# Attention: how wide the value products are, and where they stand

## The chip, the cores and the metric

The kernel runs on one core of a Trainium2 chip. The metric is the device time of one execution in microseconds (us), lower is better. PE is the core's matrix engine, DVE the vector engine, ACT the scalar engine, POOL the general engine, and SP issues most of the transfers (DMAs). A "product" below is one matmul instruction of PE.

## The reference

A decoder trunk of two layers on x of 1024 tokens by 1024 channels: layer 0 mixes by a short gated convolution, layer 1 by dilated attention, and each layer ends with a SwiGLU network. The change touches layer 1's mixer only:

```python
qkv = (h @ w_qkv).reshape(bsz, seq, 3, N_HEADS, HEAD_DIM)
q, k, v = qkv[:, :, 0], qkv[:, :, 1], qkv[:, :, 2]
for window, dilation in BRANCHES:          # (128, 1), (512, 4), (2048, 16)
    o, l = dilated_branch(q, k, v, rel_bias, window, dilation)
...
o = jnp.sum(alpha[..., None] * jnp.stack(outs, axis=0), axis=0)
return o.reshape(bsz, seq, D_MODEL).astype(h.dtype) @ w_out
```

There are 16 heads of 64 channels. Each query sees keys of three strides, with a bias by distance and a softmax over all of them. The part of the change is `v`: h (1024 by 1024) times the last third of `w_qkv` (1024 by 1024).

## The kernel before

**Numbers.** Operands are split into a high part and a low remainder, and each product of two matrices is made of three matmuls: hi times hi, hi times lo, lo times hi. A weight slab is loaded raw by SP (L153), ACT copies the high part (L139), DVE subtracts it for the low part (L140). Each is needed by its first product. SBUF is handed out in pages of 128 partitions by 1024 floats from a pool of 41 in rotation; a new tile waits for the last reader of the page that it takes.

**Order.** Nothing reorders instructions: each engine runs its own in the order in which the program writes them, and waits by semaphores for the others. The order in which weights are loaded and split is a list (`ops`); `take(key)` splits up to that key and looks a number of raw slabs ahead.

**Attention.** The normalized input h lies as eight tiles of 128 channels, each with a high and a low part. Heads go in pairs, p = 0 to 7, and the values in groups of four heads (256 columns), g = 0 to 3.

A prologue makes the keys and queries of pair 0 (`qkv(0, first=True)`) and the values of group 0 (`value_tiles(0, 0)` and `(0, 1)`). Then come slots n = 0 to 16 (`slot`), one per head and one more. Slot n makes the scores of head n (L1464, L1465) beside the products of weights with values of head n - 1 (`values`, L1537). After these, ACT evicts z and o (L1560, L1561). An odd slot (the second head of a pair) then splits the keys and queries of the next pair (`split_kq`: ACT copies to ka, kb, qa, qb, kca and kcb, L1433, and DVE's remainders, L1432). An even slot loads the values of its own pair from memory (`load_values`, L1420 and L1422, to vx). The softmax of head n is written about half way down this second part: POOL's all-reduce of the maxima (L1518) comes with the scores, then DVE subtracts (L1526) and ACT takes the exponentials (L1527) of lf, lh, ld and lp. Slot n + 1 begins with scores, and its first product with values needs lf.

Between these a slot calls `next(dense)` a set number of times, `ndense`, 27 in most slots. `dense` is the generator `qkv(p + 1)`: 36 steps for the keys and queries of the next pair (four products over eight input tiles, a step being three matmuls of 512 columns, L360 to L362, and one step for each eviction), and then steps for values: a step is six matmuls of 256 columns (L1403 to L1405), every fifth step is an eviction by ACT (L1408). At the end of an odd slot `run(dense)` drains what is left.

**Values before.** `value_tiles(g, j)` makes four tiles of 128 tokens by 256 columns, each 24 matmuls. Group 0 stands in the prologue (192 matmuls). The pairs 0 to 5 carry half a group each (96 matmuls): p = 0 and 1 group 1, 2 and 3 group 2, 4 and 5 group 3, with two weight slabs taken at each group's first half. Each page of four tiles is written to memory (`vdram`, L1412) by four DMAs on SP.

Of the kernel before, what the change touches and what calls it, by code (L numbers as in the profile page):

```python
# [3 lines left out]

# [8 lines left out]
AF = mybir.ActivationFunctionType  # L13
# [8 lines left out]
KT = D // 128  # L22
FT = DF // 128
HALF = 512
NPAIR = H // 2
# [65 lines left out]
def view(t, off, dims):  # L91
    return bass.AP(tensor=t.tensor, offset=t.offset + off, ap=[t.ap[0]] + [list(d) for d in dims])
# [3 lines left out]
def trunk(ctx: ExitStack, tc: tile.TileContext, x, gains_in, cwi, ck, cwo, wqkv, wo, relb,  # L96
          wg, wu, wd, oneh, ident, out):
    nc = tc.nc
# [6 lines left out]
    def page(name, dt=F32):  # L105
        return pages.tile([128, 1024], dt, name=name, tag="page", bufs=PAGES)
# [22 lines left out]
    def split(src, dst=None, eng=nc.vector):  # L129

        w = src.shape[1]
        if dst is None:
            if w <= HALF:
                t = page("w", F32R)
                dst = t[:, :w], t[:, HALF:HALF + w]
            else:
                dst = page("w_hi", F32R)[:, :w], page("w_lo", F32R)[:, :w]
        hi, lo = dst
        nc.scalar.activation(hi, src, AF.Copy)  # L139
        eng.tensor_tensor(out=lo, in0=src, in1=hi, op=ALU.subtract)  # L140
        return hi, lo
# [3 lines left out]
    raw_src, raw_tile, raw_state = [], {}, [0]  # L145
    ops, made, op_state = [], {}, [0, 0]
    combos, raw_base, sums_of = {}, {}, {}

    def load_raw(upto):
        while raw_state[0] < min(upto + 1, len(raw_src)):  # L150
            i = raw_state[0]
            raw_tile[i] = page("raw")
            nc.sync.dma_start(raw_tile[i][:, :raw_src[i].shape[1]], raw_src[i])  # L153
            raw_state[0] += 1

    def get_raw(i, ahead=2):
        load_raw(i + ahead)
        return raw_tile[i]
# [9 lines left out]
    def take(key, ahead=1):  # L168
        i = op_state[1]
        assert ops[i][0] == key, (ops[i][0], key)  # L170
        ensure(i + ahead)
        op_state[1] += 1
        return made.pop(i)

    def add_slab(key, src):
        i = len(raw_src)
        raw_src.append(src)
        ops.append((key, lambda: split(get_raw(i)[:, :src.shape[1]])))

    def add_pair(u, rows, w, eng, upto, low=()):  # L180

# [155 lines left out]
    for p in range(NPAIR):  # L337
        for part in (1, 0):
            add_slab(("qkv", p, part), wqkv[part * KT + p])
        if p == 0 or p % 2 and p < NPAIR - 1:  # L340
            for j in range(2):
                add_slab(("v", (p + 1) // 2, j), wqkv[2 * KT + (p + 1) // 2 * 2 + j])
    for g in range(2):
        for n in range(KT):
            add_slab(("ao", g, n), wo[n][:, g * AO * 128:(AO * 128, D)[g]])
# [996 lines left out]
        return (j // 4) * HALF + (j % 4) * 8  # L1342

    def attention(norm):
        KS, KC, QS, wv = {}, {}, {}, []

        qlo = [scope["pool"].tile([128, S], F32R, name=f"ql{a}") for a in range(2)]
        for a in range(2):
# [43 lines left out]
        def value_tiles(g, j):  # L1392

            if j == 0:
                wv[:] = [take(("v", g, i), 1) for i in range(2)]
            v = page("v")
            for b4 in range(4):
                t = 4 * j + b4
                b = bank()[:, :256]
                for k in range(KT):  # L1400
                    (hi, lo), (whi, wlo) = norm.h[k], wv[k // 4]
                    a, c = slice(t * 128, t * 128 + 128), slice(k % 4 * 256, k % 4 * 256 + 256)
                    nc.tensor.matmul(b, hi[:, a], whi[:, c], start=k == 0, stop=False)  # L1403
                    nc.tensor.matmul(b, hi[:, a], wlo[:, c], start=False, stop=False)  # L1404
                    nc.tensor.matmul(b, lo[:, a], whi[:, c], start=False, stop=k == KT - 1)  # L1405
                    if k % 2:
                        yield
                nc.scalar.activation(v[:, b4 * 256:b4 * 256 + 256], b, AF.Identity, scale=norm.r[:, t:t + 1])  # L1408
                yield
            vd = vdram[g]  # L1410
            for r in range(4):
                nc.sync.dma_start(bass.AP(vd.tensor, vd.offset + (512 * j + r) * 256,  # L1412
                                          [[16 * 256, 32], [4 * 256, 4], [1, 256]]), v[32 * r:32 * r + 32])

        def load_values(p):
            src = vdram[p // 2]
# [346 lines left out]
    with tc.tile_pool(name="first", bufs=1) as scope["pool"]:  # L1763
# [4 lines left out]
        norm = Norm(1)  # L1768
# [11 lines left out]
    with tc.tile_pool(name="third", bufs=1) as scope["pool"]:  # L1780
# [3 lines left out]
        norm = Norm(4)  # L1784
# [135 lines left out]
```

## Time and profile before

| | |
|---|---|
| median of 3 runs | 2162.24 us (2159.44 to 2163.09) |
| the profiled execution | 2161.95 us |
| its span in the trace | 2159.9 us |
| its mean granted PE clock | 0.994 |
| value products ahead of slot 0 | 192 of 256 columns |
| value products in pairs 0 to 5 | 576 of 256 columns |

The profile is of one execution of its own, so durations are compared with its time, 2161.95, which is 2 us more than the span that the trace covers. In the page's rows "x" counts instructions and "out<-in" names the tiles. A timeline row is start, duration, engine, line, operation, tiles, shapes, and in brackets the idle time just before with what ended it. A row of busy time by stretches has the stretch and its length, busy time of PE, PE's weight loads, DVE, ACT and POOL with counts, then PE's granted clock (1.00 is full), the DMA share and GB/s; where it is of one line alone, only the engines of that line stand in it.

### The profile page before, as it was taken

How to read it: one execution, taken by the hardware profiler on the slowest of the kernel's cores; microseconds unless marked ns; L12 is line 12 of the kernel's file. 1: busy time of each engine (PE TensorE's matmuls, PEld its weight loads, DVE VectorE, ACT ScalarE, POOL GpSimd, SP SyncE). 2: the span in 40 equal slices, each digit the busy share in tenths (PEclk: the TensorE clock that was granted, in tenths of full speed). 3: DMA queues.
4: the chain of work that ended last, by engine and by line, in shares of the span. 5: the costliest groups of instructions: out<-in, count | busy, mean ns of one | idle time of the engine just before them, and what ended most of it. 6: DMA issues, size and time to landing. Idle time of an engine off the chain costs nothing.

```text
span 2159.9 us, 30731 instructions
## 1 busy us (share of the span) xinstructions
PE 2128.0 (99%) x11086; PEld 1819.9 (84%) x11086; DVE 1735.9 (80%) x3166; ACT 996.4 (46%) x1792; POOL 217.7 (10%) x308
## 2 busy tenths in 40 slices
PE   8999999999999999999999999999999999999998
PEld 6788878888888888878999999887788888888887
DVE  7798758988898888865777777769988888888886
ACT  7433426444444433445455555525544444434435
POOL 2000001111211100010111111110011211200000
PEclk9999999999999999999999999999999999999999
DMA  7222543334455684323333333534224554586432
GB/s 211 69 93 67 213 150 88 127 106 163 165 173 175 233 325 145 112 64 129 92 93 93 93 93 85 172 120 167 79 88 142 175 173 164 171 317 225 160 93 79
DMA packets 148066, 306.71 MB, mean 142 GB/s; under 512 B 49850, under 2 KB 61130, under 8 KB 147914
## 3 DMA queue, kind: packets, MB, share of 16 engines
q1 hardware_dynamic: 82026, 206.83, 29.4%
q0 software_dynamic: 24720, 74.83, 10.0%
q10 hardware_dynamic: 41168, 23.10, 3.5%
q8 instruction: 88, 1.44, 0.3%
q14 instruction: 64, 0.52, 0.1%
HBM read 209.06 MB, written 88.28 MB: 138 GB/s over the span
## 4 chain that ended last, share of the span: by engine, by line
PE 86%; DVE 6%; ACT 4%; issue 2%; DMA 2%; ACTq 0%; SPq 0%; DVEq 0%
PE bank L566 18%; PE bank L567 18%; PE bank L568 18%; PE bank L362 5%; PE bank L360 5%; PE bank L361 5%; PE bank L1537 4%; PE bank L659 2%; PE bank L662 2%; PE bank L661 2%; PE bank L1465 1%; PE bank L1464 1%; PE bank L1405 1%; PE bank L1404 1%; PE bank L1403 1%
## 5 line engine op out<-in xcount | busy, mean ns | idle before, releaser
L566 PE MATMUL bank<-b,w 128*128 128x512 f32 x1816 | 712.6, 392 | 7.5 <-ACT part L572 6.7
L567 PE MATMUL bank<-b,w 128*128 128x512 f32 x1816 | 709.9, 391 | 0.6 <-DVE b L905 0.6
L568 PE MATMUL bank<-b,w 128*128 128x512 f32 x1816 | 709.0, 390 | 1.1 <-DVE w L140 1.1
L566 PEld LDWEIGHTS bank<-b,w 128*128 128x128 f32 x1816 | 342.7, 189 | 82.3 <-ACT part L572 9.0
L568 PEld LDWEIGHTS bank<-b,w 128*128 128x128 f32 x1816 | 342.3, 189 | 73.8 <-DVE w L140 2.3
L567 PEld LDWEIGHTS bank<-b,w 128*128 128x128 f32 x1816 | 342.6, 189 | 70.9 <-DVE b L905 1.2
L139 ACT ACTIVATE w<-combo 128x512 fp32r<-128x512 f32 (+2 forms) x448 | 229.3, 539 | 255.3 <-DVE combo L187 254.4
L140 DVE TENSOR_TENSOR w<-combo,w 128x512 fp32r<-128x512 f32 (+2 forms) x448 | 254.7, 581 | 27.5 <-ACT w L139 27.1
L572 ACT ACTIVATE part<-bank 128x512 f32<-128x512 f32 x168 | 100.2, 597 | 301.3 <-PE bank L568 284.9
L140 DVE TENSOR_TENSOR w<-raw,w 128x512 fp32r<-128x512 f32 (+2 forms) x312 | 172.0, 570 | 25.6 <-ACT w L139 25.3
L576 DVE TENSOR_TENSOR part<-part,bank 128x256 f32<-128x256 f32 (+1 forms) x328 | 154.2, 500 | 40.0 <-ACT part L572 26.7
L139 ACT ACTIVATE w<-raw 128x512 fp32r<-128x512 f32 (+2 forms) x312 | 152.8, 527 | 61.3 <-DMA raw<-in_ffn_w_down 16.5
L820 DVE TENSOR_TENSOR x<-x,bank 128x512 f32<-128x512 f32 x168 | 114.8, 684 | 37.4 <-PE bank L568 33.6
L360 PE MATMUL bank<-w_hi,w 128*128 128x512 f32 (+1 forms) x320 | 119.8, 374 | 2.1 <-ACT w L139 2.1
L362 PE MATMUL bank<-w_hi,w 128*128 128x512 f32 (+1 forms) x320 | 118.1, 369 | 0.7 <-DVE w L140 0.7
L361 PE MATMUL bank<-w_lo,w 128*128 128x512 f32 (+1 forms) x320 | 117.8, 368 | 0.0
L497 DVE TENSOR_TENSOR x<-x,bank 128x512 f32<-128x512 f32 (+1 forms) x104 | 66.0, 642 | 60.5 <-PE bank L362 52.2
L360 PE MATMUL bank<-h_hi,w_hi 128*128 128x512 f32 x256 | 104.5, 408 | 0.3 <-ACT w_hi L139 0.3
L187 DVE TENSOR_TENSOR combo<-raw 128x512 f32<-128x512 f32 (+1 forms) x160 | 103.2, 645 | 0.0
L362 PE MATMUL bank<-h_hi,w_lo 128*128 128x512 f32 x256 | 100.1, 391 | 0.7 <-DVE w_lo L140 0.7
L361 PE MATMUL bank<-h_lo,w_hi 128*128 128x512 f32 x256 | 99.9, 390 | 0.0
L1518 POOL PARTITION_ALL_REDUCE mb<-m x16 | 51.5, 3222 | 422.0 <-DVE m L1515 161.4
(259 smaller groups left out, 3798.9 us busy)
## 6 DMA issues: line engine op xcount, KB each, us to landing
hin<-part SPq DMA_DIRECT2D x126, 256.0 KB
raw<-in_ffn_w_gate SPq DMA_DIRECT2D x44, 512.0 KB
raw<-in_ffn_w_up SPq DMA_DIRECT2D x44, 512.0 KB
b<-ready SPq DMA_DIRECT2D x42, 512.0 KB
part<-sum POOLq DMA_DIRECT2D x72, 256.0 KB, 3.5
raw<-in_ffn_w_down SPq DMA_DIRECT2D x48, 384.0 KB
x<-spill SPq DMA_DIRECT2D x24, 512.0 KB
raw<-in_attn_w_qkv SPq DMA_DIRECT2D x24, 512.0 KB
```

What stands on the lines that cost most here:

```text
L139: nc.scalar.activation(hi, src, AF.Copy)
L140: eng.tensor_tensor(out=lo, in0=src, in1=hi, op=ALU.subtract)
L187: eng.tensor_tensor(out=c, in0=a, in1=b, op=op)
L360: nc.tensor.matmul(b, whi[:, a], ahi[:, s], start=first, stop=False)
L361: nc.tensor.matmul(b, whi[:, a], alo[:, s], start=False, stop=False)
L362: nc.tensor.matmul(b, wlo[:, a], ahi[:, s], start=False, stop=last)
L566: nc.tensor.matmul(b, hi[:, a], bhi, start=start and k == 0, stop=False, skip_group_check=True)
L567: nc.tensor.matmul(b, hi[:, a], blo, start=False, stop=False, skip_group_check=True)
L568: nc.tensor.matmul(b, lo[:, a], bhi, start=False, stop=k == n - 1, skip_group_check=True)
L572: nc.scalar.activation(t, b, AF.Copy)
L576: nc.vector.tensor_tensor(out=t, in0=t, in1=b, op=ALU.add)
L820: nc.vector.tensor_tensor(out=X[n][:, half(h)], in0=X[n][:, half(h)], in1=b, op=ALU.add)
```

## The change

Three things are changed.

Groups 0 and 1 (heads 0 to 7) are both made in the prologue, in one product of 512 columns: `wide_values` has eight tiles of 128 tokens, each 24 matmuls, with a weight slab of two input tiles by 512 columns. There are four of these slabs, each loaded by two DMAs. Each tile has one eviction of 512 columns, and two tiles fill a page, which eight DMAs write to `vdram`.

Groups 2 and 3 (heads 8 to 15) are spread over the pairs: `value_tiles(g)` is one generator for a whole group, and the run of pair p = 1 to 6 (in the slots of pair p - 1) takes 15 steps of it, that is 3, 3 and 2 tiles for each group. The weights are taken at p = 1 and p = 4.

`ndense` goes from 27 to 25 in both slots of pairs 0 to 5.

```diff
-        if p == 0 or p % 2 and p < NPAIR - 1:
+        if p == 0:
+            for j in range(4):
+                add_wide(("v", 0, j), [wqkv[2 * KT + g * 2 + j // 2][:, j % 2 * HALF:j % 2 * HALF + HALF]
+                                       for g in range(2)])
+        if p in (1, 4):
             for j in range(2):
-                add_slab(("v", (p + 1) // 2, j), wqkv[2 * KT + (p + 1) // 2 * 2 + j])
+                add_slab(("v", 2 + p // 4, j), wqkv[2 * KT + (2 + p // 4) * 2 + j])
...
             if first:
-                yield from value_tiles(0, 0)
-            n = p - 1
-            if first or n < NPAIR - 2:
-                yield from value_tiles(0 if first else n // 2 + 1, 1 if first else n % 2)
+                yield from wide_values()
+            elif p < NPAIR - 1:
+                if p % 3 == 1:
+                    tiles[0] = value_tiles(2 + p // 4)
+                yield from islice(tiles[0], 15)
+
+        def wide_values():
+
+            w = [take(("v", 0, i), 1) for i in range(4)]
+            for t in range(8):
+                b = bank()
+                v = page("v") if t % 2 == 0 else v
+                for k in range(KT):
+                    (hi, lo), (whi, wlo) = norm.h[k], w[k // 2]
+                    a, c = slice(t * 128, t * 128 + 128), half(k % 2)
+                    nc.tensor.matmul(b, hi[:, a], whi[:, c], start=k == 0, stop=False)
+                    nc.tensor.matmul(b, hi[:, a], wlo[:, c], start=False, stop=False)
+                    nc.tensor.matmul(b, lo[:, a], whi[:, c], start=False, stop=k == KT - 1)
+                    yield
+                nc.scalar.activation(v[:, half(t % 2)], b, AF.Identity, scale=norm.r[:, t:t + 1])
+                if t % 2:
+                    for r in range(4):
+                        for g in range(2):
...
+                            nc.sync.dma_start(bass.AP(vd.tensor, vd.offset + row * 256,
+                                                      [[16 * 256, 32], [4 * 256, 2], [1, 256]]),
+                                              view(v[32 * r:32 * r + 32], g * 256, [[HALF, 2], [1, 256]]))
+                yield
...
-            slot(2 * p, dense, 24 if last else 29 if p == NPAIR - 2 else 27, 3 if last else 0, hook)
+            slot(2 * p, dense, 24 if last else 29 if p == NPAIR - 2 else 25, 3 if last else 0, hook)
             run(hook)
-            slot(2 * p + 1, dense, 22 if last else 27)
+            slot(2 * p + 1, dense, 22 if last else 27 if p == NPAIR - 2 else 25)
```

How the order moves on ACT in the prologue, from the first splits of pair 0's keys and queries. In brackets stand the semaphores waited for (DMA queues, DVE, PE, ACT itself, Pool for POOL); w_hi is the high part of a weight slab. Before:

```order
L1433 ACTIVATE qa<-kq 64x512 [waits DMAHW7_49,DVE_49]
L1433 ACTIVATE qb<-kq 64x512 [waits DMAHW0_49]
L139 ACTIVATE w_hi<-raw 128x1024 [waits DMAHW6_49]
L1433 ACTIVATE qa<-kq 64x512
L1433 ACTIVATE qb<-kq 64x512
```

And with the change, whose split_kq is L1474:

```order
L1474 ACTIVATE qa<-kq 64x512 [waits DMAHW1_49,DVE_49]
L1474 ACTIVATE qb<-kq 64x512 [waits DMAHW2_49]
L139 ACTIVATE w_hi<-raw 128x1024 [waits DMAHW1_49,DMAHW0_49]
L139 ACTIVATE w_hi<-raw 128x1024 [waits DMAHW5_49,DMAHW3_49,DMAHW2_49]
L139 ACTIVATE w_hi<-raw 128x1024 [waits DMAHW4_49,DMASW1_49,Activation_49]
L1474 ACTIVATE qa<-kq 64x512
L1474 ACTIVATE qb<-kq 64x512
```

Where one weight slab stood behind the first four copies, three do: slabs 2 and 3 of the wide product, and the next pair's first.

ACT in the odd slot of pair 1 (slot 3), from the first split copy behind the evictions to the first exponential. Before:

```order
L1433 ACTIVATE qa<-kq 64x512 [waits DVE_49,Activation_49]
L1433 ACTIVATE qb<-kq 64x512 [waits Pool_49]
L1433 ACTIVATE qa<-kq 64x512
...
L1433 ACTIVATE qb<-kq 64x512
L1408 ACTIVATE v<-bank,r 128x256 [waits DMAHW1_49,DMAHW6_49,DVE_49,PE_49]
L1433 ACTIVATE qa<-kq 64x512
L1433 ACTIVATE qb<-kq 64x512
L1433 ACTIVATE kca<-ka 128x512 [waits DVE_49]
L1433 ACTIVATE kcb<-kb 128x512 [waits DVE_49]
L1527 ACTIVATE lf<-lf 128x1024 [waits DVE_49]
```

And with the change, where the exponentials are L1568:

```order
L1474 ACTIVATE qa<-kq 64x512 [waits Activation_49,Pool_49]
L1474 ACTIVATE qb<-kq 64x512 [waits PE_49]
L1474 ACTIVATE qa<-kq 64x512
...
L1474 ACTIVATE qb<-kq 64x512
L1474 ACTIVATE qa<-kq 64x512
L1474 ACTIVATE qb<-kq 64x512
L1474 ACTIVATE kca<-ka 128x512 [waits DVE_49]
L1474 ACTIVATE kcb<-kb 128x512 [waits DVE_49]
L1568 ACTIVATE lf<-lf 128x1024 [waits DVE_49]
```

The eviction of a value tile that stood among the copies now stands behind the exponentials, and the wait for POOL has moved from qb to qa, one copy earlier.

More of the change, by code (lines that the diff above doesn't have):

```diff
@@ L1 @@
 import math
-from itertools import chain
+from itertools import chain, islice
 from contextlib import ExitStack
@@ L147, in trunk, with load_one @@
     combos, raw_base, sums_of = {}, {}, {}
+    def load_one(i):
+        raw_tile[i] = page("raw")
+        src = raw_src[i]
+        if isinstance(src, list):
+            for g, s in enumerate(src):
+                nc.sync.dma_start(view(raw_tile[i], g * 256, [[HALF, 2], [1, 256]]),
+                                  bass.AP(s.tensor, s.offset, [s.ap[0], [256, 2], [1, 256]]))
+            return
+        nc.sync.dma_start(raw_tile[i][:, :src.shape[1]], src)
     def load_raw(upto):
         while raw_state[0] < min(upto + 1, len(raw_src)):
-            i = raw_state[0]
-            raw_tile[i] = page("raw")
-            nc.sync.dma_start(raw_tile[i][:, :raw_src[i].shape[1]], raw_src[i])
+            load_one(raw_state[0])
             raw_state[0] += 1
@@ L1386, in qkv, with value_tiles @@
             if first:
-                yield from value_tiles(0, 0)
-            n = p - 1
-            if first or n < NPAIR - 2:
-                yield from value_tiles(0 if first else n // 2 + 1, 1 if first else n % 2)
[L1392 to L1398, printed above, removed]
+                yield from wide_values()
[19 more added lines that the diff above has]
+                        for g in range(2):
+                            vd = vdram[g]
+                            row = 512 * (t // 4) + 4 * (t % 4 - 1) + r
+                            nc.sync.dma_start(bass.AP(vd.tensor, vd.offset + row * 256,
+                                                      [[16 * 256, 32], [4 * 256, 2], [1, 256]]),
+                                              view(v[32 * r:32 * r + 32], g * 256, [[HALF, 2], [1, 256]]))
+                yield
+        def value_tiles(g):
+            wv = [take(("v", g, i), 1) for i in range(2)]
+            for t in range(8):
+                j, b4 = divmod(t, 4)
+                v = page("v") if b4 == 0 else v
                 b = bank()[:, :256]
@@ L1408, in value_tiles @@
                 nc.scalar.activation(v[:, b4 * 256:b4 * 256 + 256], b, AF.Identity, scale=norm.r[:, t:t + 1])
+                vd = vdram[g]
+                for r in range(4 * (b4 == 3)):
+                    nc.sync.dma_start(bass.AP(vd.tensor, vd.offset + (512 * j + r) * 256,
+                                              [[16 * 256, 32], [4 * 256, 4], [1, 256]]), v[32 * r:32 * r + 32])
                 yield
[L1410 to L1413, printed above, removed]
         def load_values(p):
```

6 lines of the change are left out of this document (5 added, 1 removed).

## The prediction

> **What bounds the kernel now.** I read the page first, then busy time by stretches, then the timelines of PE, ACT and POOL around the places where values are computed.
>
> ```profile
> span 2159.9 us, 30731 instructions
> PE 2128.0 (99%) x11086; PEld 1819.9 (84%) x11086; DVE 1735.9 (80%) x3166; ACT 996.4 (46%) x1792; POOL 217.7 (10%) x308
> ...
> PE 86%; DVE 6%; ACT 4%; issue 2%; DMA 2%; ACTq 0%; SPq 0%; DVEq 0%
> ```
>
> PE is busy for 99% of the span and holds 86% of the chain that ended last; ACT is busy for under half and still holds 4% of it. So two questions decide: how many us of PE work the change adds or removes, and whether PE still has work wherever something is taken from it. The attention part shows the price of a value product (stretches of the 256 column products alone, a third of them: line L1403 is one of the three lines of each product):
>
> ```profile
> 1007.30:1030.80 23.50, 18.50 (x64) 12.28 (x64) 1.00 0.10 23
> 1120.00:1131.70 11.70, 9.05 (x32) 6.00 (x32) 1.00 0.12 46
> ```
>
> The first row is the prologue ahead of slot 0: 3 x 64 = 192 products. The second is slot 3: 3 x 32 = 96. Slot 3 is an odd slot, and its end, from the last product of the values with the weights (L1537) to the first of the next slot, reads so on PE:
>
> ```profile
> 1116.60 0.47 PE L360 MATMUL bank<-h_hi,w_hi 128*128 128x512 f32 x1
> 1116.91 0.39 PE L361 MATMUL bank<-h_lo,w_hi 128*128 128x512 f32 x1
> ...
> 1119.86 0.39 PE L362 MATMUL bank<-h_hi,w_lo 128*128 128x512 f32 x1
> 1120.09 0.28 PE L1403 MATMUL bank<-w_hi,h_hi 128*128 128x256 f32 x1
> ...
> 1131.48 0.28 PE L1405 MATMUL bank<-w_hi,h_lo 128*128 128x256 f32 x1
> ...
> 1132.30 0.28 PE L1464 MATMUL bank<-qa,kca 128*128 128x256 f32 x1
> ...
> 1132.99 1.16 PE L1537 MATMUL bank<-lf,vx 128*128 128x128 f32 x8
> ```
>
> and on ACT and POOL:
>
> ```profile
> 1118.63 0.63 ACT L1433 ACTIVATE kb<-kq 64x512 fp32r<-64x512 f32 x1
> 1119.28 0.63 ACT L1433 ACTIVATE qa<-kq 64x512 fp32r<-64x512 f32 x1
> 1121.34 0.63 ACT L1433 ACTIVATE qb<-kq 64x512 fp32r<-64x512 f32 x1 [1.43 <-POOL mb L1518]
> ...
> 1127.98 0.47 ACT L1408 ACTIVATE v<-bank,r 128x256 f32<-128x256 f32 x1
> ...
> 1131.88 1.05 ACT L1527 ACTIVATE lf<-lf 128x1024 f32<-128x1024 f32 x1
> ```
> ```profile
> 1118.08 3.23 POOL L1518 PARTITION_ALL_REDUCE mb<-m  x1 [22.28 <-DVE m L1515]
> ```
>
> The first exponential ends at 1131.88 + 1.05 = 1132.93, and PE's first product that needs it starts at 1132.99. ACT has gone from the last product's eviction through the split copies of keys and queries to that exponential with a single wait (1.43 us for POOL's all-reduce). So the end of an odd slot has two limits of equal length: PE's products and ACT's row of copies. Taking PE work out of it gains nothing that ACT doesn't give up as well.
>
> **What a product costs, narrow and wide.** 96 products of 256 columns go from 1120.09 to 1131.60 (the last starts at 1131.48 and takes one step): 11.51 us, 0.120 each. From the first L361 at 1116.91 to the last L362 of that stretch at 1119.86 lie 13 steps of 512 columns (five triples, of which these are the second and the fifteenth): 2.95 us, 0.227 each. So two narrow ones cost 0.240 and a wide one 0.227. The change turns 384 narrow ones (groups 0 and 1) into 192 wide ones: 46.1 against 43.6 us, a saving of 2.5 us in all, 0.1%. The Trainium skill, "Perfetto Trace Analysis", section on optimizing tensor performance, says of matmuls that larger ones are more efficient where possible; the rows agree, but by 5% only.
>
> **Prologue: +20.5 us of PE work, and a new wait of 3.3.** Before, 192 narrow products, 23.04 us; now 192 wide ones, 43.58 us, and nothing runs beside them that leaves the path: +20.5. Their evictions (ACT, one of 512 columns per token tile) and writes hide beside the products. The splits of the weight slabs do not. The order of ACT puts the high parts of slabs 2 and 3 behind four split copies, where one slab stood before; that slab's rows, and the first value product:
>
> ```profile
> 1007.44 0.68 PE L1403 MATMUL bank<-w_hi,h_hi 128*128 128x256 f32 x1
> ```
> ```profile
> 1011.07 0.63 ACT L1433 ACTIVATE qb<-kq 64x512 fp32r<-64x512 f32 x1
> 1011.72 1.06 ACT L139 ACTIVATE w_hi<-raw 128x1024 fp32r<-128x1024 f32 x1
> ```
> ```profile
> 1012.81 1.23 DVE L140 TENSOR_TENSOR w_lo<-raw,w_hi 128x1024 fp32r<-128x1024 f32 x1 [1.84 <-ACT w_hi L139]
> ```
>
> A wide slab holds two of the eight input tiles, so slab 2 is due after 12 products. The first starts at 1007.44 and takes 0.40 longer than the usual 0.28 of the L1403 row above; then 12 x 0.227 gives 1010.57. Its low part is there at 1012.81 + 1.23 = 1014.04. One product (hi times hi) fits in between, so PE waits 3.47 - 0.23 = 3.25 us. Slab 3 follows one split later, at about 1015.3, and is due at 1016.8: no wait. Bounds: 0, if the splits come to stand earlier than the copies before them allow; 4.5, if slab 3 costs another split of 1.23.
>
> Slot 0 then needs the values back from memory. The writes on SP's queue are eight per two tiles, not four per four:
>
> ```profile
> 1024.51 2.58 SPq L1412 DMA_DIRECT2D vdram<-v  x4
> ```
> ```profile
> 1045.61 1.06 ACT L1527 ACTIVATE lf<-lf 128x1024 f32<-128x1024 f32 x1 [1.33 <-DVE lf L1526]
> ```
> ```profile
> 1051.52 0.72 PE L1537 MATMUL bank<-lf,vx 128*128 128x128 f32 x5
> ```
>
> At 0.65 us each the last group takes 2.6 longer, while the first exponential of slot 0 ends 1051.52 - 1046.67 = 4.85 ahead of its use. This costs nothing; the bound if the cover were gone is 2.6.
>
> **Slots: 23.0 us of products leave, 8.6 come back.** Pairs 0 to 5 lose 24, 24, 48, 24, 24, 48 narrow products (3, 3, 2, 3, 3, 2 tiles where 4 were), 192 in all, 23.0 us. All of them leave the end of an odd slot, since the generator is drained there. The numbers 27 to 25 work the other way: a slot takes two steps less, one eviction step and one step of three products. So 3 x 0.227 = 0.68 us leaves the even slot and 0.68 the first part of the odd one, and six products move to the odd slot's end. Each of the twelve slots is bound by PE where these stand: -8.2 us that are real.
>
> The odd slots' ends before: slot 3 has 1132.99 - 1116.60 = 16.39. Slot 1 reads
>
> ```profile
> 1062.82 0.47 PE L360 MATMUL bank<-h_hi,w_hi 128*128 128x512 f32 x1
> ...
> 1078.99 0.38 PE L1537 MATMUL bank<-lf,vx 128*128 128x128 f32 x2
> ```
> ```profile
> 1070.22 1.04 ACT L139 ACTIVATE w_hi<-raw 128x1024 fp32r<-128x1024 f32 x1
> ...
> 1077.66 1.05 ACT L1527 ACTIVATE lf<-lf 128x1024 f32<-128x1024 f32 x1
> ```
>
> 16.17, bound by PE; ACT's row there, with a weight split and no wait for POOL, ends at 1078.71, so alone it would give 15.95 (with the 0.06 from exponential to product). Slots 5 and 9 I take to be like slot 1, slots 7 and 11 like slot 3: 3 x 16.17 + 3 x 16.39 = 97.7.
>
> After: PE's own work is 16.17 + 6 x 0.227 - 24 x 0.120 = 14.65 with three tiles and 11.77 with two. ACT's row loses the value eviction (0.47), which now comes behind the exponentials. In pairs 1, 2, 4 and 5 it keeps the wait for POOL, and by the order the copy that waits is qa and not qb: the all-reduce ends at the same time and one more copy (1119.28 - 1118.63 = 0.65) stands behind it. That gives 16.39 - 0.47 + 0.65 = 16.57. In pairs 0 and 3, with a weight split and no such wait, 15.95 - 0.47 = 15.48. Sum 2 x 15.48 + 4 x 16.57 = 97.2. The ends of the odd slots give back 0.4 us, and PE idles there instead: 0.8 in pairs 0 and 3, 1.9 in 1 and 4, 4.8 in 2 and 5, where it falls in two pieces, one ahead of the score products that wait for the split keys and one ahead of the first exponential. Bounds: -17 us if ACT's row were short enough for PE to be the limit everywhere, +2 if a second copy came to stand behind the all-reduce in those four pairs.
>
> One short wait at some slots' starts also goes, by the order three such places become two (waits in the stretch from 1007 to 1350 us: total, times, longest):
>
> ```profile
> PE bank L1464 <- ACT o L1561: 1.8, 3, 0.6
> ```
>
> that is -0.6. **Sum with PE's clock as it is:** 20.5 + 3.25 - 8.2 - 0.4 - 0.6 = +14.6, and 2161.95 + 14.6 = 2176.5. The base is the profiled execution (span 2159.9 and 2 us around it), 0.3 us below the median of the runs, 2162.24.
>
> **PE's clock.** Windows of 3.41 us from elsewhere in the trace (busy PE first, granted clock third from the end), and products in them:
>
> ```profile
> 46.68:50.09 3.41, 1.32 (x6) 0.75 (x4) 3.41 (x6) 2.78 (x5) 0.09 (x1) 1.00 0.39 70
> 50.09:53.50 3.41, 3.25 (x8) 2.58 (x9) 3.41 (x7) 2.40 (x6) 1.60 (x2) 0.50 0.65 119
> 954.62:958.03 3.41, 2.75 (x13) 1.94 (x11) 1.45 (x6) 1.99 (x4) 0.51 (x1) 1.00 0.07 13
> 958.03:961.44 3.41, 3.03 (x12) 2.22 (x13) 1.95 (x4) 1.45 (x3) 2.40 (x3) 1.00 0.14 26
> ```
> ```profile
> 45.02 0.63 PE L566 MATMUL bank<-b,w 128*128 128x512 f32 x1
> 45.44 0.63 PE L567 MATMUL bank<-b,w 128*128 128x512 f32 x1
> ...
> 50.24 0.79 PE L566 MATMUL bank<-b,w 128*128 128x512 f32 x1 [2.24 <-ACT part L572]
> ```
>
> After a window with PE busy for 1.32 of 3.41 and one wait of 2.24, the next window has half the clock; the one after 2.75 busy has all of it. At half the clock a 512 column product steps by 0.42 instead of 0.227, so a full window loses 3.41 x (1 - 0.227 / 0.42) = 1.57 us. New waits of that size are the prologue's (3.25) and those of pairs 2 and 5 (4.8 each): three halved windows, about 1.5 each, +4.5. Those of pairs 1 and 4 (1.9) lie between the two rows; I take none of them, and up to 1.5 each for the range. So 2176.5 + 4.5 = **2181**. The Trainium skill, "TensorE: Matmul & The Clock Gate", sections "What's actually happening" and "Why this matters for your kernels", has the clock drop after an idle window of some 3.4 us and warns of gaps above 3; no run here shows that limit as such, the row of 2.24 speaks for a lower one. By the page the pieces in pairs 2 and 5 would cost nothing and the sum would be 2176.5 to 2178.
>
> **Rivals.** *The clock stays full.* A halved window needs more idle than the new waits put into one window. For it: windows have fixed edges, and 3.25 us across an edge leaves under 2.1 in each; none of the halved windows above lies in attention. Against it: 2.24 was enough. Time 2176.5.
>
> *No wait in the prologue.* Slab 2's split gets done before PE needs it, if ACT gets to it sooner than in the rows. For it: ACT there waits on data that may arrive otherwise. Against it: its order is fixed, four copies first. 2173 to 2176 with the clock's share.
>
> *More halved windows.* Pairs 1 and 4 drop too, or pairs 2 and 5 twice: 2184 to 2188.
>
> *The other side: PE stays the limit at the odd slots' ends.* If ACT's row from the last product to the first exponential took under 14.65 us (11.77 in pairs 2 and 5), all 23.0 us would come back: 20.5 - 23.0 - 0.6 = -3.1 without the prologue's wait, 2158.8, and +0.1 with it, 2162. For it: ACT is busy 46% overall. Against it: the exponential ended 0.06 us ahead of its use, and the row of copies behind POOL's all-reduce has no gap that the change could close.
>
> **How the numbers follow.** The forecast, three halved windows give or take one, has 0.45; full clock 0.25; no prologue wait 0.12; more halved windows 0.10; PE as the limit 0.08, of which 0.02 ends below the bound for faster. 0.2%, 4.3 us, is about what a measurement of this kernel can tell from no change; from the four cases on the slow side none ends within it. That makes faster 0.02, same 0.06, slower 0.92. The range runs from the case without the prologue's wait, 2172, to one with more halved windows, 2187; what lies outside is PE as the limit and the rest of the halved windows.
>
> **What would show it.** Right: in the prologue PE waits about 3.3 us for the low part of a weight slab (L140) after 12 wide products, and the prologue's value products take some 24 us longer than before; the wide step is 0.227; odd slots' ends of 15.5 in pairs 0 and 3 and 16.6 in the others, with PE waiting for split keys and the first exponential; ACT's qa waits for POOL where qb did; granted clock 0.50 in the window after those waits. Wrong: odd slots' ends near 12 to 14.6 us, with exponentials ended long ahead of PE; no wait of PE in the prologue; a clock of 1.00 throughout; or waits at a place that I gave none, such as slot 0's first product with the values, waiting for their way through memory.

## The result, and the profile after

The changed kernel takes 2187.06 us (median of 4 runs, 2184.35 to 2190.29) against 2162.18 for the kernel before: ratio 1.0117, 95% interval 1.0105 to 1.0129. It is slower by some 25 us, where 19 were forecast, and lies just above the range of 2172 to 2187. The profiled execution, 2190.29, is the longest of the four, 28.3 us above that of before (2161.95).

The head of the page of the changed kernel:

```profile
span 2188.5 us, 30393 instructions
...
PE 2135.8 (98%) x10894; PEld 1818.0 (83%) x10894; DVE 1734.7 (79%) x3166; ACT 994.9 (45%) x1784; POOL 217.0 (10%) x308
```

There are 192 products fewer, and yet PE is busy for longer and for a smaller share. What PE waited for between 1000 and 1420 us (line, what it waited for; total, times, longest):

```profile
PE bank L1578 <- ACT lf L1568: 14.5, 6, 3.0
PE bank L1505 <- ACT qa L1474: 2.6, 2, 1.3
PE bank L1419 <- ACT w_hi L139: 2.0, 1, 2.0
PE bank L1420 <- DVE w_lo L140: 0.8, 1, 0.8
PE bank L1505 <- ACT o L1602: 0.6, 1, 0.6
```

There are six waits for the first exponential, one per odd slot's end, and the two for qa stand ahead of the scores in pairs 2 and 5. Before, PE had none of these; its one row in the same stretch was:

```profile
PE bank L1464 <- ACT o L1561: 2.3, 4, 0.6
```

Busy time in the prologue from the first value product on, and at the odd ends of pairs 0, 1 and 2:

```profile
1006.60:1055.66 49.06, 46.27 (x194) 37.31 (x193) 12.06 (x15) 20.38 (x28) 0.00 (x0) 0.97 0.12 32
1086.24:1103.82 17.58, 15.10 (x104) 13.68 (x102) 12.31 (x15) 15.10 (x21) 3.22 (x1) 0.99 0.25 81
1140.70:1157.30 16.60, 14.82 (x104) 13.66 (x102) 13.26 (x17) 14.35 (x21) 3.79 (x2) 1.00 0.09 36
1194.30:1210.90 16.60, 12.28 (x79) 10.77 (x78) 13.27 (x18) 14.36 (x21) 3.77 (x2) 0.95 0.10 39
```

In the prologue PE stands still for 2.8 us. At the odd ends it is busy for 15.1, 14.8 and 12.3 us of ends that last 17.6, 16.6 and 16.6.

The stretches of the two traces follow one another without gaps, so they can be set against the forecast's terms. An odd end here runs from the start of a slot's last product of L1537 (L1578 now) to the first of the next slot, 0.03 us more than in the prediction.

| stretch | before | after | difference | forecast |
|---|---|---|---|---|
| first value product to first score | 23.43 | 48.98 | +25.6 | +20.5 +3.25 +1.5 |
| even slots' ends, six (first one from the first score) | 20.65, 14.19 x5 | 19.94, 13.51 x5 | -4.1 | -8.2 with the next row |
| odd slots' products with values, six | 11.27 | 10.60 | -4.0 | |
| odd ends of pairs 0 and 3 | 16.20, 16.42 | 17.58, 17.58 | +2.5 | -1.6 |
| odd ends of pairs 1, 2, 4 and 5 | 16.42, 16.20, 16.20, 16.42 | 16.62, 16.57, 16.61, 16.57 | +1.1 | +1.2 |
| products with values behind the odd ends | 12.11, 11.39, 12.11, 11.38, 12.11, 12.21 | 12.76, 12.94, 13.71, 12.94, 11.39, 14.23 | +6.6 | -0.6 +3.0 |
| all else | | | +0.6 | 0 |
| sum | | | +28.3 | +19.0 |

Two rows are off: the odd ends of pairs 0 and 3, by 4 us, and the products behind the odd ends, by 4 us.

**The prologue** went as forecast in its sum, 25.6 for 25.25. PE's waits are 2.8 us and not 3.25, and 2.04 of them are for the slab's high part on ACT, where the prediction had named the low part. The products for slab 2 on PE:

```profile
1012.05 0.50 PE L1419 MATMUL bank<-w_hi,h_hi 128*128 128x512 f32 x1 [2.04 <-ACT w_hi L139]
1013.31 0.50 PE L1420 MATMUL bank<-w_lo,h_hi 128*128 128x512 f32 x1 [0.76 <-DVE w_lo L140]
```

**Odd end of pair 0.** ACT, DVE and PE in slot 1:

```profile
1096.20 1.06 ACT L139 ACTIVATE w_hi<-raw 128x1024 fp32r<-128x1024 f32 x1
...
1099.33 1.15 ACT L1474 ACTIVATE kca<-ka 128x512 fp32r<-128x512 f32 x1 [0.76 <-DVE ka L1473]
...
1102.68 1.06 ACT L1568 ACTIVATE lf<-lf 128x1024 f32<-128x1024 f32 x1 [1.18 <-DVE lf L1567]
```
```profile
1097.29 1.23 DVE L140 TENSOR_TENSOR w_lo<-raw,w_hi 128x1024 fp32r<-128x1024 f32 x1 [4.21 <-ACT w_hi L139]
1098.55 0.69 DVE L1473 TENSOR_TENSOR ka<-kq,ka 64x512 fp32r<-64x512 f32 x1
...
1101.42 1.23 DVE L1567 TENSOR_TENSOR lf<-lf,mb 128x1024 f32<-128x1024 f32 x1
```
```profile
1103.79 0.80 PE L1578 MATMUL bank<-lf,vx 128*128 128x128 f32 x2 [2.44 <-ACT lf L1568]
```

Before, the weight split of this end stood ahead of the second half's copies, on ACT (behind the high part of 1070.22) and on DVE:

```profile
1071.17 0.61 ACT L1433 ACTIVATE ka<-kq 64x512 fp32r<-64x512 f32 x1
```
```profile
1071.29 1.23 DVE L140 TENSOR_TENSOR w_lo<-raw,w_hi 128x1024 fp32r<-128x1024 f32 x1 [1.84 <-ACT w_hi L139]
...
1075.42 1.23 DVE L1526 TENSOR_TENSOR lf<-lf,mb 128x1024 f32<-128x1024 f32 x1
```

Now it stands four copies later. DVE idles 4.21 us for the slab's high part, makes the low part, and only then its remainders for ka, kb and ql, behind which its subtraction for lf is queued. ACT waits 0.76 for ka and 1.18 for lf: the chain has left ACT and runs over DVE.

**Odd end of pair 1.** ACT's wait has moved to qa, as forecast:

```profile
1145.49 0.63 ACT L1474 ACTIVATE qa<-kq 64x512 fp32r<-64x512 f32 x1 [1.99 <-POOL mb L1559]
```

**The clock.** Windows of 3.41 us, each with the one that follows: the prologue's wait, the end of pair 2, the end of pair 4:

```profile
1011.16:1014.58 3.42, 1.78 (x6) 1.23 (x7) 2.55 (x3) 3.38 (x5) 0.00 (x0) 1.00 0.00 0
1014.58:1017.99 3.41, 3.41 (x9) 2.65 (x8) 3.30 (x5) 2.27 (x3) 0.00 (x0) 0.50 0.00 0
1205.73:1209.14 3.41, 0.85 (x5) 0.54 (x4) 3.32 (x6) 3.31 (x6) 0.00 (x0) 1.00 0.01 2
1209.14:1212.55 3.41, 1.64 (x7) 1.65 (x8) 2.92 (x6) 3.41 (x5) 0.00 (x0) 0.50 0.00 0
1318.36:1321.78 3.42, 1.80 (x12) 1.66 (x13) 2.86 (x5) 3.42 (x6) 0.00 (x0) 1.00 0.00 0
1321.78:1325.19 3.41, 3.41 (x31) 3.37 (x30) 1.75 (x4) 1.63 (x5) 0.00 (x0) 1.00 0.30 72
```

The granted clock halves behind the prologue's wait and behind the ends of pairs 0, 1, 2, 3 and 5, and behind pair 4 it doesn't. Behind pairs 2 and 5 two windows in a row are halved. The products that start there read 12.76 to 14.23 against 11.39 behind pair 4.

### The profile page after: what moved, and what is told of

It reads as the page before. It is cut to its first block, busy times and chain, and to the rows that moved or that the text cites. A ratio compares the mean times of both kernels' runs of the same rounds, so it can differ in the third digit from the quotient of the medians.

```text
span 2188.5 us, 30393 instructions
## 1 busy us (share of the span) xinstructions
PE 2135.8 (98%) x10894; PEld 1818.0 (83%) x10894; DVE 1734.7 (79%) x3166; ACT 994.9 (45%) x1784; POOL 217.0 (10%) x308
## 4 chain that ended last, share of the span: by engine, by line
PE 81%; DVE 7%; ACT 6%; issue 3%; DMA 2%; POOL 0%; ACTq 0%; SPq 0%; DVEq 0%; POOLq 0%
PE bank L583 17%; PE bank L585 17%; PE bank L584 17%; PE bank L379 5%; PE bank L377 5%; PE bank L378 5%; PE bank L1578 4%; PE bank L676 2%; PE bank L679 2%; PE bank L678 2%; PE bank L1506 1%; PE bank L1505 1%; DVE w L140 1%; DVE x L514 1%; DMA x<-spill 1%
## 5 line engine op out<-in xcount | busy, mean ns | idle before, releaser
L140 DVE TENSOR_TENSOR w<-raw,w 128x512 fp32r<-128x512 f32 (+2 forms) x312 | 171.6, 568 | 25.6 <-ACT w L139 25.4
```

## The experiments

The theory after the two traces (A): PE's work is not the limit of the odd ends; rows of copies on ACT and, in pairs 0 and 3, DVE are; and the time that PE idles there costs twice, since its clock halves behind it. The rivals: PE's order is the limit throughout, or the halved clock costs nothing, or values made so early cost something by themselves. The kernel before stood between 2160.3 and 2161.0 in these comparisons, so ratios and differences to it are compared, not times; the changed kernel stands at +24.9. Stretches are those of the table above.

**e1: the prologue's splits earlier.**

```diff
         for i, _ in enumerate(qkv(0, first=True)):
+            if i == 30:
+                ensure([k for k, f in ops].index(("v", 0, 3)))
             if i == 4 * (KT + 1) - 1:
                 later = split_kq(0)
```

> The changed kernel, with the splits of wide slabs 2 and 3 issued before the split copies of pair 0's keys and queries. Theory A (the prologue's wait is the splits' place in ACT's order, and the halved clock behind it follows from the wait): PE's waits of 2.0 and 0.8 us for w_hi and w_lo go, the halved window at 1014.6 goes too (1.6), so the stretch from the first value product to the first score falls from 49.0 to about 44.4 and the time by some 4.4 us, to 2182 to 2183. Theory B (the raw slabs arrive late, or the splits only push the copies and slot 0 waits for them instead): the wait stays or moves, less than 2 us gained.

2183.02 us, +22.7 to before: ratio 1.0102 (1.0087 to 1.0117). The prologue from the first value product on (the first 43.9 of 43.96 us):

```profile
1007.57:1051.50 43.93, 43.93 (x194) 36.23 (x193) 9.78 (x13) 18.31 (x26) 0.00 (x0) 1.00 0.13 36
```

PE has no idle time left and the full clock: 43.96 against 48.98, 5.0 us less, as theory A has it, and 192 products of 0.227 fill it. The median, against before, fell by 2.2 only, and the intervals of the two ratios overlap. Halved windows behind the odd ends fall differently from run to run (here behind four ends, one of them pair 4's), which may be why. The stretch is what shows the step.

**e2: the next pair's split earlier in pairs 0 and 3.**

```diff
-                w = take(("qkv", p, part), 2 - part)
+                w = take(("qkv", p, part), 3 if part == 0 and p in (1, 4) else 2 - part)
```

> The changed kernel, with the split of the next pair's first slab in pairs 0 and 3 moved from the middle of the odd slot's copies to the even part of the pair. Theory A (DVE's low part of that slab stands ahead of its remainders for keys and queries, so the exponential waits for DVE there): the odd slots' ends of pairs 0 and 3 fall from 17.58 to 15.5 us, the waits of ACT for ka (0.76) and lf (1.18) go, and the halved clock behind them too; time 4 to 8 us less, 2179 to 2183. Theory B (ACT's copies alone set the end, the slab's 1.06 us on ACT is all it costs): 1.1 us each, 2185. Theory C (the end is set by something else in PE's order): no change.

2177.2 us, +16.9: ratio 1.0076 (1.0061 to 1.0091), 8 us less than the change has above before. ACT and PE at the end of slot 1:

```profile
1098.72 1.14 ACT L1474 ACTIVATE kcb<-kb 128x512 fp32r<-128x512 f32 x1
1099.77 1.05 ACT L1568 ACTIVATE lf<-lf 128x1024 f32<-128x1024 f32 x1
```
```profile
1101.01 1.05 PE L1578 MATMUL bank<-lf,vx 128*128 128x128 f32 x8
```

Neither ACT nor PE waits there now. The ends of pairs 0 and 3 are 14.68 both, 2.9 us shorter (theory A had expected 2.1): with the split away PE's own sum of 14.65 is the limit, so the detour over DVE and the split's own time on ACT both went. The halved windows behind these two ends are gone as well (11.27 and 11.27 after 12.76 and 12.94). The other four ends stand at 16.6.

**e3: PE's idle time covered with work that nothing reads.**

```diff
                 yield from islice(tiles[0], 15)
+                spare = bank()[:, :256]
+                count = (36, 18, 12)[p % 3]
+                for k in range(count):
+                    nc.tensor.matmul(spare, norm.h[k % KT][0][:, 0:128], norm.h[k % KT][0][:, 128:384],
+                                     start=k == 0, stop=k == count - 1)
```

> The changed kernel, with spare products of 256 columns added behind the last value product of each odd slot's end, 18 in pairs 0 and 3, 12 in 1 and 4, 36 in 2 and 5: 132 in all, 15.8 us of PE work that nothing reads. Theory A (PE idles there 2 to 5 us, and the idle time halves its clock in the window behind): the odd slots' ends stay at 16.6 to 17.6, the halved windows in the slots go, and the time falls by 5 to 9 us in spite of the added work, to 2178 to 2182. Theory B (the idle is on the path for another reason, and the clock's windows cost nothing): no change. Theory C (PE's products bound the odd slots' ends): slower by up to 16 us, 2203.

2181.58 us, +21.3: ratio 1.0097 (1.0082 to 1.0112), with 132 products more. The waits of PE in the slots' stretch, first row:

```profile
PE bank L1583 <- ACT lf L1573: 2.6, 6, 0.6
```

The odd ends are 17.58, 16.66, 16.63, 17.59, 16.66 and 16.63, as without the added work; so 15.8 us of products fit into PE's idle time, and PE isn't the limit there. No window in the slots is halved, and the six stretches of products behind them read 11.46, 11.39, 11.39, 11.47, 11.38 and 12.23: 8.6 us less than in the changed kernel. That is what the clock cost in the slots of the profiled execution, the longest of its four; the median, against before, fell by 3.6 only.

**e4: kca and kcb on DVE.**

```diff
-                    copy(kc[:, s], view(kt, h * HALF, [[1, 4], [4, 128]]))
+                    nc.vector.tensor_copy(kc[:, s], view(kt, h * HALF, [[1, 4], [4, 128]]))
```

> The changed kernel, with the copies kca and kcb (four of 1.05 us in each odd slot's end) moved from ACT to DVE. Theory A (ACT's row of copies sets the odd slots' ends, PE's own work there is 14.65 or 11.8 us): the ends fall by 2 to 4 us each, to 14.7 in pairs 1 and 4 and to 13 to 14 in 2 and 5, and most halved windows go: 12 to 24 us less, 2163 to 2175. Theory B (DVE is as long as ACT there, 0.7 us and more for each copy): the ends stay within 1 us, 2181 to 2187. Theory C (PE's order bounds): no change.

2184.62 us, +24.3: ratio 1.0116 (1.0099 to 1.0133), no difference to the changed kernel. The ends of pairs 1, 2, 4 and 5 fell to 15.3, by 1.3 each, where theory A had 2 to 4; those of pairs 0 and 3 rose to 17.94 and 19.05. In slot 1 on DVE and on ACT, and the first exponential of slot 3:

```profile
1089.55 0.62 DVE L1488 CAST kcb<-kb 128x512 fp32r<-128x512 f32 x1
...
1091.52 0.69 DVE L1386 SCALAR_TENSOR_TENSOR kq<-bank,rstd 128x512 f32<-128x512 f32 x1
...
1099.83 1.23 DVE L1567 TENSOR_TENSOR lf<-lf,mb 128x1024 f32<-128x1024 f32 x1
```
```profile
1092.24 0.63 ACT L1474 ACTIVATE qa<-kq 64x512 fp32r<-64x512 f32 x1 [1.40 <-DVE kq L1386]
...
1101.09 1.06 ACT L1568 ACTIVATE lf<-lf 128x1024 f32<-128x1024 f32 x1 [5.18 <-DVE lf L1567]
```
```profile
1152.01 1.06 ACT L1568 ACTIVATE lf<-lf 128x1024 f32<-128x1024 f32 x1 [2.62 <-DVE lf L1567]
```

The copies are shorter on DVE (0.62), but they stand ahead of the eviction of kq that ACT needs (1.40 us of waiting) and of the subtraction for lf (5.18). ACT's row is the limit in four ends, by 1.3 us only, and DVE's is the next: with the copies moved, the exponential of slot 3 waits 2.62 us for DVE. Theory A is right about what bounds the four but not about the gain; B is right about the others and about the time.

**e5: value products taken out of the kernel before.** In the groups 1 to 3, a quarter of the token tiles has 3 products where 24 stood, so their values are wrong.

```diff
-                    nc.tensor.matmul(b, hi[:, a], whi[:, c], start=k == 0, stop=False)
+                    if g == 0 or b4 < 3 or k == 0:
+                        less = g and b4 == 3
+                        nc.tensor.matmul(b, hi[:, a], whi[:, c], start=k == 0, stop=False)
...
```

> The kernel before, with 21 of the 96 value products of each of the pairs 0 to 5 left out (126 in all, 15.1 us of PE work; those values are wrong, everything else stays). Theory A (PE's products and the row of copies on ACT are equally long at the odd slots' ends before, so work taken from there gains only what PE was longer): the ends stay at 16.0 to 16.4 us, 1 to 2 us faster in all, 2159 to 2161, PE idle there 2 us each; a halved clock behind it may make it no faster at all. Theory B (PE is the limit everywhere, as its 99% of busy time says): 15 us faster, 2146.

2164.85 us, +4.1: ratio 1.0018 (1.0009 to 1.0028), slower with 126 products less. Its page, its waits of PE in the stretch of the slots, and two windows:

```profile
PE 2116.3 (98%) x10960; PEld 1807.3 (84%) x10960; DVE 1736.5 (80%) x3166; ACT 996.2 (46%) x1792; POOL 217.0 (10%) x308
```
```profile
PE bank L1539 <- ACT lf L1529: 13.9, 6, 2.5
```
```profile
1182.20:1185.61 3.41, 1.31 (x12) 1.10 (x11) 3.08 (x5) 3.41 (x5) 0.00 (x0) 1.00 0.00 0
1185.61:1189.02 3.41, 3.41 (x15) 3.13 (x15) 0.06 (x1) 3.32 (x7) 0.00 (x0) 0.50 0.00 0
```

The odd ends are 15.95, 16.38, 15.94, 16.37, 15.94 and 16.38, where 16.20 and 16.42 stood: 0.9 us gained of the 15.1 taken out. 13.9 us of it became waits for the first exponential, and three windows behind them are halved: the products there take 13.79, 12.99 and 13.79 where 12.11, 11.38 and 12.11 stood, 5.0 us more. That is why the time lies above the 2159 to 2161 of theory A. This shows by itself, without a wide product and without a longer prologue, that value products taken from these ends give nothing back.

**e6: 27 steps again.**

```diff
-            slot(2 * p, dense, 24 if last else 29 if p == NPAIR - 2 else 25, 3 if last else 0, hook)
+            slot(2 * p, dense, 24 if last else 29 if p == NPAIR - 2 else 27, 3 if last else 0, hook)
...
-            slot(2 * p + 1, dense, 22 if last else 27 if p == NPAIR - 2 else 25)
+            slot(2 * p + 1, dense, 22 if last else 27)
```

> The changed kernel with the 27 steps of before in the slots of pairs 0 to 5, not 25. Theory A (six products per pair go back from the odd slots' ends, where PE idles, to stretches where PE is the limit): each even slot's gap and each odd slot's products take 0.68 us more, the odd ends stay within 0.5 of 16.6 and 17.6: 8 us slower than the changed kernel, about 2195, and with more halved windows up to 2200. Theory B (PE's order is the limit throughout): no change, 2187.

2199.98 us, +39.2: ratio 1.018 (1.0162 to 1.0199), 14 us worse than the changed kernel. Each even slot's end and each odd slot's products take 0.68 us more, as theory A has it, and all six odd ends are followed by a halved window. The ends of pairs 0 and 3 missed: 15.94, not 17.6. ACT in slot 1:

```profile
1097.29 1.04 ACT L139 ACTIVATE w_hi<-raw 128x1024 fp32r<-128x1024 f32 x1
...
1100.84 0.47 ACT L1449 ACTIVATE v<-bank,r 128x256 f32<-128x256 f32 x1
...
1102.63 1.14 ACT L1474 ACTIVATE kca<-ka 128x512 fp32r<-128x512 f32 x1
...
1104.69 1.05 ACT L1568 ACTIVATE lf<-lf 128x1024 f32<-128x1024 f32 x1
```

With two steps more per slot the split stands earlier again and nothing waits for DVE. The value eviction (0.47) is back among the copies too, and the end is ACT's row of before, 15.94 for the 15.95 in the prediction; without that eviction it would be the prediction's 15.48. The other four ends are 17.03 to 17.09, longer than 16.6 by the same eviction. So the 25 steps have three effects: six products move, the value eviction goes behind the exponentials, and in pairs 0 and 3 the split comes later.

**e7: the prologue's values as two narrow groups.**

```diff
             if first:
-                yield from wide_values()
+                yield from value_tiles(0)
+                yield from value_tiles(1)
```

> The changed kernel, with the values of heads 0 to 7 in the prologue made as two groups of 256 columns and not in one of 512. Theory A (a wide product saves 5% of two narrow ones, and its slabs' splits come too late, which the narrow slabs' don't): the stretch from the first value product to the first score has 384 x 0.120 = 46.1 us of products and no wait, against 49.0 with the wide ones: 2 to 3 us faster than the changed kernel, 2184. Theory B (the wide product is worth more than its waits): slower, 2189 or above.

2186.2 us, +25.4: ratio 1.0119 (1.0104 to 1.0134), the same as with the wide product. From the first value product to the first score, and its one wait of PE:

```profile
1008.17:1056.11 47.94, 46.99 (x386) 46.35 (x385) 12.15 (x15) 22.36 (x36) 0.00 (x0) 1.00 0.21 56
```
```profile
PE bank L1445 <- DVE w_lo L140: 0.9, 1, 0.9
```

47.94 us where theory A had 46.1 and no wait: 1.0 less than the wide one with its waits and its halved window, and 4.0 more than the wide one without them (e1). The width's own gain is small, and its splits took it back.

**e8, e9 and e10: the parts put right together.** e8 has the edits of e1 and e2, 24 and 22 steps in the second and third pair of a group (even and odd slots alike), and steps are drawn early where the split needs a query that isn't made:

```diff
+                while a == 1 and i in (0, 3) and p + 1 < NPAIR and (0, i // 3) not in parts[p + 1]:
+                    next(dense)
...
-            slot(2 * p, dense, 24 if last else 29 if p == NPAIR - 2 else 25, 3 if last else 0, hook)
+            slot(2 * p, dense, 24 if last else 29 if p == NPAIR - 2 else (25, 24, 22)[p % 3], 3 if last else 0, hook)
...
```

> The changed kernel with all that the first runs showed put right: the prologue's splits and the next pair's split early, and the steps per slot 25, 24, 22 in the three pairs of a group, so that PE's idle time at the odd slots' ends is filled with products of the slots. From the stretches: prologue +20.6, two steps less per slot -8.1, waits gone -2.2, the further steps moved -10.9, odd ends 2 x 14.7 + 4 x 16.6 against 97.7 before, -2. Theory A (these are all the causes, and none of them is the wide product or its place): within 4 us of the kernel before, 2157 to 2163. Theory B (making half of all values ahead of slot 0 costs something that the slots can't give back whatever stands there): 2170 or above.

2169.87 us, +9.1: ratio 1.0046 (1.0029 to 1.0063). Theory A's number missed by 7 us, and the time stands at the border of theory B. The expectation had counted steps taken from odd slots, which only move inside their own end; the even ends fell by 0.68 and 2.04, and 0.67 of that came back in the odd slot's products of pairs 2 and 5. So 4.1 us moved, not 10.9, and the ends that should have been filled still wait: 17.0 and 17.3, 0.4 and 0.75 longer than in the changed kernel. ACT in slots 3 and 5:

```profile
1135.16 0.63 ACT L1474 ACTIVATE qa<-kq 64x512 fp32r<-64x512 f32 x1 [2.36 <-POOL mb L1559]
```
```profile
1187.29 0.63 ACT L1474 ACTIVATE qb<-kq 64x512 fp32r<-64x512 f32 x1 [0.76 <-PE bank L378]
```

In slot 3 the wait for POOL is 2.36 where it was 1.99, and in slot 5 there is a new wait of 0.76, for a product of the queries: these are the whole difference. e9 takes the steps from even slots alone, (25, 22, 17):

> The mended kernel with fewer steps in the even slots alone: 25, 22, 17 in the three pairs of a group, 25 in the odd ones (a step less in an odd slot only moved work inside its own end). Theory A (the 9 to 10 us of PE's idle time at the odd ends of pairs 1, 2, 4 and 5 can be filled by products from the even slots): 2 x (3 + 8) steps of 0.68 us against the changed kernel's 25, of which the mended kernel had taken 2 x 4; some 9 us less than its 2169.9, 2160, and no halved windows in the slots. Theory B (the queries' products then end too late for their copies, and the ends grow by what the slots lose): 2167 or above.

2165.14 us, +4.2: ratio 1.0021 (1.0011 to 1.003). Its waits of PE:

```profile
PE bank L1578 <- ACT lf L1568: 6.8, 4, 2.2
PE bank L1505 <- ACT o L1602: 0.6, 1, 0.6
```

The even ends fell to 11.47 and 8.75; the odd ends rose to 17.4 and 18.9. The slots gave up 12.3 us and the ends took back 6.3, so half of it is theory A, half B: work can move into the ends, up to where the queries' products come too late for their copies. e10 has the edit of e4 too and (25, 23, 19):

> The mended kernel with the copies kca and kcb on DVE, and 25, 23, 19 steps in the even slots. Theory A (ACT's row is 1.3 us shorter in pairs 1, 2, 4 and 5, and PE's idle time there is filled): ends of about 14.7, 15.7 and 16, 2 x (2 + 6) steps moved: 2157 to 2161, level with the kernel before or 0.1% below it. Theory B (DVE takes ACT's place in pairs 0 and 3, as in the first run with these copies): ends of 16 and more there, 2164 or above.

2166.92 us, +5.9: ratio 1.0024 (1.0015 to 1.0034), a miss. The odd ends of pairs 1 and 4 are 16.0, close to the 15.7 expected, but 17.8 in pairs 2 and 5 and 15.48 in pair 3, and there are two halved windows.

**e11: the kernel before with kca and kcb on DVE,** the edit of e4.

> The kernel before with the copies kca and kcb on DVE. Theory A (ACT's row and PE's products are equally long there): the odd ends of pairs 1, 3 and 5 fall from 16.4 to PE's 16.2, at most 1 us in all, 2160 to 2162, no change that can be measured. Theory B (DVE becomes the longer row, as in pairs 0 and 3 of the changed kernel): ends of 17 us and more, 2165 or above. Theory C (ACT's row was the limit before as well): 2150 to 2155.

2161.91 us, ratio 1.0001 (0.9992 to 1.0011). The odd ends of pairs 1, 3 and 5 fell from 16.42 to 16.20, as theory A has it, and those of pairs 2 and 4 rose from 16.20 to 16.55 and 16.61: in the kernel before PE and ACT really are equally long, and shortening one alone gains nothing. No version run here is faster than the kernel before.

## Why the prediction was wrong

Its direction and its mechanism held; the size was too small by a quarter, in two terms. The measured time is that of its rival *More halved windows* (2184 to 2188), and that rival holds in part: pair 1 dropped, and pairs 2 and 5 twice, but it had nothing of pairs 0 and 3.

*What bounds the odd ends*: right. Two limits of equal length, so work taken from one of them gains nothing; e5 shows it with the kernel before alone (0.9 of 15.1 us), e3 with the changed one (15.8 us of products added, and the ends as long as without them).

*The prologue, +20.5 and 3.25*: right, 25.6 in all for 25.25, with some luck in the parts. Without wait and halved window it is +20.5 (e1); the other 5.0 are waits of 2.8, for 3.25, and 2.2 beyond them, for the 1.5 of a halved window. Wide products step by 0.227 as said; e1's stretch is 192 of them.

*Two steps less, -8.2*: right, -8.1, and e6 gives it back.

*Odd ends of pairs 1, 2, 4 and 5*: right, 16.6 for 16.57, with the wait at qa.

*"In pairs 0 and 3, with a weight split and no such wait, 15.95 - 0.47 = 15.48"*: **this step failed.** The ends are 17.58, and the two of them cost 4 us more than forecast. The step took ACT's row of before, where the split stands ahead of the second half's copies, and subtracted an eviction. It didn't look at where the split stands after the change, four copies later, and that DVE's low part goes ahead of remainders that ACT waits for. e2 takes the split out and the ends fall to 14.68; e6 puts it earlier and they fall to 15.94, with the eviction of 0.47 in them. So the subtraction was sound, and the split's place was not.

*"Three halved windows, about 1.5 each"*: **too few.** Of the new waits at odd ends two were counted, and five of six were followed by half the clock in the profiled execution, over seven windows: 8.6 us (e3) for 3.0. Those of pairs 0 and 3 are the failed step's: they idle for 2.4 us and not 0.8, and with e2 their halved windows go. The one of pair 1 was left at nothing between two rows.

*The short wait, -0.6*: with no window halved (e3), the products that had it show 0.7 less each at three places, -2.1. That works the other way and hides some of the misses.

*The rival in which PE stays the limit* is excluded by e3 and e5. The one with a full clock is, too, by the granted clock of 0.50 behind five of the six odd ends. The Trainium skill, "TensorE: Matmul & The Clock Gate", section "What's actually happening", has the clock drop after an idle window of some 3.4 us; the window of 1205.73 had 0.85 us of products in it, and its successor has half the clock. The measurement decides here.

What stays open: what decides the clock near the border, since a window with 1.78 us of products (1011.16) was followed by half of it, and windows with 1.80 (1318.36) and, in e9, 1.54 by all of it.

## What to carry to other kernels

Before taking work from an engine that is 99% busy, look at what ends last at the place that it is taken from: where another engine's row is as long, the work is paid for and the time isn't given back, and a clock that follows PE's activity can make less work slower (e5: 126 products less, 4.1 us more). When a change shifts a generator's steps, follow every instruction that rides on it, weight splits above all, to its new place on each engine's queue, and ask which later instruction on that queue someone waits for. An added cost at one place and a saving at another only cancel if both are on the path; here the prologue's 20.5 us were, and the 23.0 at the odd slots' ends were not.

## What the runs showed of the hardware

A window that is only partly idle can halve the clock of the next one: of the windows shown, those with 0.85, 1.31, 1.32 and 1.78 us of products in 3.41 were followed by 0.50, those with 1.80 and 2.75 by 1.00. The busy time alone doesn't decide it. In e9 one with 1.54 kept the full clock:

```profile
1348.24:1351.65 3.41, 1.54 (x11) 1.46 (x12) 3.10 (x6) 3.41 (x5) 0.00 (x0) 1.00 0.00 0
1351.65:1355.06 3.41, 3.41 (x31) 3.36 (x30) 1.50 (x4) 1.53 (x4) 0.00 (x0) 1.00 0.14 34
```

In the trace of before, one with 2.76 us (at 74.00) was followed by 0.50.

The windows' edges aren't tied to the program: the halved window of the same prologue starts 7.89 us behind the first value product in the changed kernel, 7.59 in e2 and 5.31 in e3. So the same odd end is hit in one run and not in another (pair 4 in e1 and not in the changed kernel). The changed kernel's four times spread over 6 us; whether that comes from this, no run tests.

In e7's prologue the loads of PE's weights take 0.19 us each and follow one another at the products' step of 0.120, so they overlap; they are busy for 46.35 of 47.94 us. In e1's wide one they take 0.19 us as well, at a step of 0.227, and are busy for 36.23 of 43.93. Whether that is why two narrow products cost 5% more than a wide one, no run tested by itself.
